# The first projection of a two-layer backbone, taken a quarter of the features at a time, and two pairs of modulation sums in one room

## The chip, the cores and the metric

The kernel runs on one core of one Trainium2 chip. The metric is device microseconds (us) of one execution. The kernel before took 1750.79 us, the median of three runs (1748.19 to 1751.60).

## What is computed

The reference is two layers of a diffusion backbone over 512 latent tokens `x` and 256 context tokens `ctx`, each of 1024 features in float32. The latents are modulated by a vector `c`, the context by another, `c_ctx`. Cut to the part that matters here:

```python
sc, scc = jax.nn.silu(c), jax.nn.silu(c_ctx)
m_lat = split(sc  @ mod_w[0] + mod_b[0], 6)      # six vectors of 1024: shift, scale, gate, twice
m_ctx = split(scc @ mod_w[0] + mod_b[0], 6)
h_ctx = rms(x_ctx) * norm_pre_mix * (1 + m_ctx[1]) + m_ctx[0]
h_lat = rms(x_lat) * norm_pre_mix * (1 + m_lat[1]) + m_lat[0]
h = concat([h_ctx, h_lat])                        # 768 tokens
gq, gk, gv, gog, gz, aq, ak, av = split(h @ w_in, (256, 256, 512, 512, 32, 512, 128, 128))
logit = gz[d] @ gla_w_gate[d] + gla_b_gate[d]     # d: forward, backward
g = log_sigmoid(logit) / 16                       # forget gates
# chunkwise gated linear recurrence in both directions over gq, gk, gv, g;
# softmax attention over aq, ak, av; both side by side through w_out
x_lat = x_lat + m_lat[2] * rms(o_lat @ w_out)
h_lat = rms(x_lat) * norm_pre_ffn * (1 + m_lat[4]) + m_lat[3]
# ... a gated FFN, and a second layer of another kind
```

## The kernel before

**Engines and tiles.** TensorE (PE) does the products and the transposes; VectorE (DVE) and ScalarE (ACT) move its results out of PSUM and do the element work; SyncE (SP) issues most loads. The dense products are float32 made of three products each: an operand X is split into a high part H (a cast, on ACT) and a low part L = X - H (a subtraction, on DVE), and `mm3` (above `gemm_T`) adds up H·H, H·L and L·H. A weight comes in 0.52 MB units: `unit` takes a `raw` tile (three of them), loads it on SP, casts it to `wH` (line 699, ACT) and makes `wL` (line 700, DVE); there are four `wH` and four `wL` for the whole program. PSUM has tiles by tag: two `mm` of 1024 columns, `sc0` and `sc1`, and two `tr` of 512.

**What sets the order.** Each engine takes its instructions in one list. A scheduler orders what isn't pinned; while `self.pinned` is set, what goes through `pin` (matmuls, transposes and what else is wrapped) keeps program order. Behind the head of the program that order is written by hand: each stage is a generator, and `run` steps them as a string of names says, one step for each name (`"Q Q e m"`). Buffers, PSUM tiles included, make the rest: who takes a tile waits until its last user is done.

**The head** (`run`, lines 1655 to 1706). `constants` loads the small vectors and turns them into columns `col` with one PE transpose, then makes `scT`, the two modulation vectors through silu. Six token tiles `xt` of 128 x 1024 are loaded, normed (sum of squares on ACT, scaling on DVE, line 1659) and transposed by PE into `xT` (eight blocks of 128 features by 768 tokens, copies at line 1666). Then two halves of the features follow: eight loads of `mod_w` (`mraw`, 128 x 1024, nine buffers), 32 narrow products into `mod_acc00`, four column groups side by side; `mod_cols` copies the rows out (line 485) and transposes them, and adds the bias (line 497); line 1694 makes the scale `aff01`; lines 1703 and 1705 apply shift and scale to that half of `xT`; `put` splits it into the high and low parts `x0`, `x1` of `h` (lines 665 and 666). Between the halves the units for the first product, 288 columns wide, are taken.

**The first layer's mixer** (`even_mixer`). Its first product `nat` computes the gate rank z (32 columns) and half of the queries for three pairs of token tiles, context first. `decays` transposes z and calls `gla_gates` (`logit`, then lines 1228 on). `mod_vec` computes the two next pairs of modulation vectors not on PE but on DVE: for each of eight 128-row slices of a weight, `macc = macc + mraw * scT` at line 554 (line 552 for the first slice), 128 x 1024, once for the latents and once for the context; then PE adds the 128 rows up with a column of ones (`mod_acc`), and `mod_cols` turns them into columns. The first pair, `macc020` and `macc021`, is the gate of the mixer; `gate_rows` makes its products with `norm_post_mix` and turns them into rows (`gc02` on line 600, `gt02` on line 606). The second pair, `macc030` and `macc031`, is the FFN's shift. Both pairs have accumulators of their own (`sums=4`), and the weight slices four buffers.

The string before the scan steps the q and k columns of the first two heads (`qk0`, evacuated as `gqk0`, `gqk2`), their values (`v0`, into `gvo`), the gates (`e`), modulation (`m`), the other queries (`q`) and keys with values (`kv`). The next string begins with the scan (`c0`, `l0`), whose first operands `arrg` are made on DVE (line 1248) and whose first product on PE is named `pcg`; between its steps stand the rest of `kv`, `qk1` and `v1`.

Of the kernel before, what the change touches and what calls it, by code (L numbers as in the profile page):

```python
# [17 lines left out]
P = 128  # L18
D = 1024
# [320 lines left out]
class Net:  # L340
# [3 lines left out]
    def __init__(self, ctx, tc, I, out):  # L344
        self.tc, self.nc, self.I, self.out = tc, tc.nc, I, out
        tc.nc.scalar.preload_act_table_set("silu_and_others")
# [41 lines left out]
    def constants(self):  # L388
# [11 lines left out]
        self.col_rows(  # L400
            "rows", 0, P, (
# [6 lines left out]

        nc.gpsimd.memset(self.scT, 0.0)
        nc.scalar.activation(  # L410
            self.scT[:, :, 0:2].rearrange("p k r -> p r k"),
            self.col[:, R_C : R_C + 16].rearrange("p (r k) -> p r k", r=2),
            AF.Silu,
        )
        self.modcol, self.gates = {}, {}

    def col_rows(self, nm, r0, r1, parts):

        rows = self.wp.tile([P, WU], F32, tag="mraw", bufs=2, name=nm)[: r1 - r0, :P]
        for at, src, n in parts:  # L420
            self.nc.scalar.dma_start(out=rows[at - r0 : at - r0 + n, :], in_=src)
        pt = self.tr_tile(f"pt_{nm}")
        self.tr(pt[:, 0 : r1 - r0], rows, self.ident[0 : r1 - r0, 0 : r1 - r0])
        self.nc.vector.tensor_copy(self.col[:, r0:r1], pt[:, 0 : r1 - r0])

    def late_constants(self):
        nc, I, cst = self.nc, self.I, self.cst
        self.col_rows(
            "rows2", R_NQM, R_END, (
# [10 lines left out]
        mf = self.wp.tile([P, WU], F32, tag="mraw", bufs=2, name="masks_f")[:, :160].rearrange("p (m i) -> p m i", m=5)  # L440
        nc.scalar.dma_start(out=mf, in_=I["const_masks"])
        nc.vector.tensor_copy(self.masks, mf)
# [30 lines left out]
    def mod_loads(self, l, ms, k, pool, bufs):  # L473
        us = []
        for m in ms:
            u = (pool or self.wp).tile([P, WU], F32, tag="mraw", bufs=bufs, name=f"mraw{l}{m}{k}")
# [54 lines left out]
    def mod_vec(self, pool, jobs, own=None, bufs=2, sums=2, single=False):  # L531
# [4 lines left out]
        load = lambda l, k, m: self.mod_loads(l, (m,), k, own, bufs)[0]  # L536
        u = load(*steps[0])
        i = 0
        for l, ms, then in jobs:
            self.mod_tiles(l, [m for m, r in ms if r == 0])  # L540
            accs = [pool.tile([P, D], F32, tag="macc", bufs=sums, name=f"macc{l}{m}{r}") for m, r in ms]
            while i < len(steps) and steps[i][0] == l and steps[i][2] in [m for m, _ in ms]:
                k, m = steps[i][1:]
                i += 1
                ahead = load(*steps[i]) if i < len(steps) else None
                here = [(a, r) for a, (mm, r) in zip(accs, ms) if mm == m]
                for x, (a, r) in enumerate(here):
# [3 lines left out]
                    if k == 0:  # L551
                        nc.vector.tensor_scalar(a, u, w, None, op0=ALU.mult)
# [505 lines left out]
    def even_mixer(self, h, mix, zu, last):  # L1058
# [24 lines left out]
        with self.tc.issue_after(last):  # L1083
            self.gemm_nat(w, 1536, 288, h, tiles, ev_z, us=zu)
# [779 lines left out]
```

## Time and profile before

| | before |
|---|---|
| median of three runs | 1750.79 us (1748.19 to 1751.60) |
| the profiled execution | 1749.34 us, of which its span is 1747.5 |
| mean granted TensorE clock | 0.993 of full speed |
| HBM read, written | 175.66 MB, 9.46 MB |
| first product of the mixer, first score of the scan | at 37.63 us and 133.98 us of the span |

All times inside the program are of the profiled execution and count from the start of its span. A row of the table by windows gives a stretch, its length, the busy time of PE, of its weight loads (PEld), DVE, ACT and POOL with the instruction counts in brackets, then the mean granted clock, the share of the time in which the 16 DMA engines were busy (a mean) and GB/s. A timeline row gives start, duration, engine, line, operation and tiles, and in square brackets the idle time just before it with what ended it. A row of the groups gives the count, the busy time in all, the mean in ns, and the idle time before. Line 371 is the helper through which every matmul and transpose passes, so PE's groups are told apart by their tiles. In "1328.47:1331.68 3.21, 0.01 (x1)" PE did 0.01 us of work in a stretch of 3.21 us.

### The profile page before, as it was taken

The numbers are of one execution on the slowest core, as the hardware profiler recorded it, in microseconds if no ns is written. First come the engines' busy times: TensorE is split into PE (matmuls) and PEld (weight loads), VectorE is DVE, ScalarE is ACT, GpSimd is POOL, SyncE is SP. The second block draws the span as 40 slices with busy tenths as digits, with TensorE's granted clock in tenths as the row PEclk, the third lists the DMA queues.
The fourth block names the chain that finished last, engine by engine and source line by source line (L and its number), as shares of the span: only waits on it lengthen the run. The fifth ranks groups of instructions, "written<-read, shape, count | busy, mean of one in ns | idle before, by whom it ended". The sixth has DMA issues, their size and how long they took to land. (4 is left out here: it accounts for less than half of the span.)

```text
span 1747.5 us, 32790 instructions
## 1 busy us (share of the span) xinstructions
PE 1700.9 (97%) x13732; PEld 1526.0 (87%) x13732; DVE 1280.9 (73%) x2036; ACT 857.8 (49%) x1473; POOL 74.2 (4%) x93
## 2 busy tenths in 40 slices
PE   6999999999999999999999999999999999999998
PEld 4889986788999989989998988889898899989997
DVE  5879658735966979787668658787764678878785
ACT  5545557746543333333347336666644664344342
POOL 1004100001000000000001000000000100000000
PEclk8999999999999999999999999999999999999999
DMA  8731013154322424332234752121114333233333
GB/s 318 222 112 39 3 39 107 36 156 139 113 90 73 153 77 156 109 110 61 73 123 143 262 160 63 48 62 50 50 62 133 121 98 108 86 102 106 99 106 120
DMA packets 169647, 187.23 MB, mean 107 GB/s; under 512 B 6262, under 2 KB 140956, under 8 KB 169500
## 3 DMA queue, kind: packets, MB, share of 16 engines
q1 hardware_dynamic: 167568, 181.56, 32.8%
q10 hardware_dynamic: 1932, 3.59, 0.7%
q8 instruction: 107, 1.75, 0.4%
q14 instruction: 40, 0.33, 0.1%
HBM read 175.66 MB, written 9.46 MB: 106 GB/s over the span
## 5 line engine op out<-in xcount | busy, mean ns | idle before, releaser
L371 PE MATMUL nat<-wH,x 128*128 128x256 f32 (+1 forms) x1216 | 229.0, 287 | 0.4 <-issue 0.4
L754 ACT CAST wH<-raw 128x1024 fp32r<-128x1024 f32 x120 | 124.5, 1051 | 197.2 <-PE acc L371 86.2
L700 DVE TENSOR_TENSOR wL<-raw,wH 128x1024 fp32r<-128x1024 f32 (+1 forms) x126 | 151.3, 1206 | 84.3 <-ACT wH L699 83.9
L371 PEld LDWEIGHTS nat<-wH,x 128*128 128x128 f32 x1216 | 193.3, 193 | 3.8 <-ACT y L1329 0.8
L755 DVE TENSOR_TENSOR wL<-raw,wH 128x1024 fp32r<-128x1024 f32 x120 | 145.2, 1221 | 64.9 <-ACT wH L754 64.8
L699 ACT CAST wH<-raw 128x1024 fp32r<-128x1024 f32 (+1 forms) x126 | 128.9, 1038 | 127.8 <-PE nat L371 34.4
L371 PE MATMUL nat<-wL,x 128*128 128x256 f32 (+1 forms) x608 | 173.4, 285 | 0.0
L371 PE MATMUL acc<-wH,gH 128*128 128x512 f32 x440 | 171.8, 390 | 0.0
L371 PE MATMUL acc<-wH,gL 128*128 128x512 f32 x440 | 171.5, 390 | 0.0
L371 PE MATMUL acc<-wL,gH 128*128 128x512 f32 x440 | 171.5, 390 | 0.0
L847 DVE TENSOR_TENSOR y<-y,acc 128x1024 f32<-128x1024 f32 x135 | 115.2, 863 | 37.0 <-PE acc L371 32.8
L554 DVE SCALAR_TENSOR_TENSOR macc<-mraw,scT,macc 128x1024 f32<-128x1024 f32 x98 | 122.6, 1277 | 10.7 <-DMA mraw<-in_mod_w_dram 10.4
L371 PE MATMUL ff<-x,wH 128*128 128x512 f32 (+1 forms) x512 | 127.6, 340 | 0.0
L624 POOL TENSOR_TENSOR rs<-ms,neghalf 128x1 f32<-128x1 f32 (+2 forms) x62 | 58.0, 937 | 1543.2 <-DVE ms L622 1543.1
L371 PEld LDWEIGHTS nat<-wL,x 128*128 128x128 f32 x608 | 117.3, 193 | 0.0
L371 PE MATMUL oproj<-wH,x 128*128 128x512 f32 x320 | 102.5, 397 | 3.2 <-ACT x L1270 3.2
L371 PEld LDWEIGHTS acc<-wH,gL 128*128 128x128 f32 x440 | 82.6, 188 | 17.3
L371 PEld LDWEIGHTS acc<-wH,gH 128*128 128x128 f32 x440 | 82.7, 188 | 16.6
L371 PEld LDWEIGHTS acc<-wL,gH 128*128 128x128 f32 x440 | 82.7, 188 | 16.5
L371 PEld LDWEIGHTS ff<-x,wH 128*128 128x128 f32 x512 | 87.3, 190 | 10.1
L955 ACT COPY qkh<-arr 128x512 f32<-128x512 f32 x112 | 70.1, 642 | 36.3 <-DVE arr L960 32.1
L371 PE MATMUL ff<-x,wL 128*128 128x256 f32 (+1 forms) x256 | 86.2, 337 | 0.0
(344 smaller groups left out, 4047.2 us busy)
## 6 DMA issues: line engine op xcount, KB each, us to landing
mraw<-in_mod_w_dram SPq DMA_DIRECT2D x96, 512.0 KB, 4.8
raw<-in_ffn_w_gate_dram SPq DMA_DIRECT2D x44, 512.0 KB, 3.7
raw<-in_ffn_w_up_dram SPq DMA_DIRECT2D x44, 512.0 KB, 3.8
raw<-in_ffn_w_down_dram SPq DMA_DIRECT2D x44, 512.0 KB, 3.6
raw<-in_odd_w_in_dram SPq DMA_DIRECT2D x40, 512.0 KB, 3.7
raw<-in_even_w_in_dram SPq DMA_DIRECT2D x16, 512.0 KB, 4.6
x<-xr SPq DMA_DIRECT2D x14, 512.0 KB, 2.6
xr<-x SPq DMA_DIRECT2D x14, 512.0 KB, 8.1
```

The costliest lines, as they stand in the source:

```text
L371: return self.pin(self.nc.tensor.matmul(*a, **k))
L554: nc.vector.scalar_tensor_tensor(a, u, w, a, op0=ALU.mult, op1=ALU.add)
L624: nc.gpsimd.tensor_tensor(rs, ms, self.neghalf.to_broadcast([P, w]), op=ALU.pow)
L699: nc.scalar.copy(H[:, :m], raw[:, :m])
L700: nc.vector.tensor_tensor(L[:, :m], raw[:, :m], H[:, :m].bitcast(F32), op=ALU.subtract)
L754: self.nc.scalar.copy(H, f)
L755: self.nc.vector.tensor_tensor(L, f, H.bitcast(F32), op=ALU.subtract)
L847: nc.vector.tensor_tensor(y, y, pt, op=ALU.add)
L955: nc.scalar.copy(qkv[:, :, :, half, :], dst)
```

## The change

**The head by quarters.** The six token tiles move from the pool of the head into a pool of their own, `xr`: four rooms of tag `x0` for the latents, two of tag `x1` for the context. Their norms run two tiles ahead of their transposes; the transposes of the constants (`finish`, `late`) and the load of the silu table come later than before. Matmuls, transposes and the casts marked with `pin` keep program order from here on. `begin_loads` takes a quarter of the modulation weights (256 features of shift and of scale, in two tiles of 128 x 2048, rows of 1 KB), `begin_weights` a quarter of the rows of the projection's columns for `gqk0`, `gqk2` and `v0` as one unit of 128 x 1024. `begin` then goes through the quarters: `sums` is the 32 narrow products, now 128 wide, `columns` the transpose, bias, `aff01`, shift, scale and split of that quarter's two feature blocks, `across` the products for `gqk0` and `gqk2`, `values` those for `v0`, and `gates` the gate rank z as 64 narrow products, 32 rows by 192 columns, into free columns of `gqk0`'s PSUM tile. All five PSUM tiles (two `mm`, `sc0`, `sc1`, one `tr`) hold their sums through the four quarters; `md`, for the modulation, is `sc0` ahead of quarter one and the other `tr` after that. When the quarters are done, `even_mixer` copies them out, and the queries that stood first (`Q`) come next, with the weights `wq` taken in quarter four.

**The second pair of sums.** `mod_vec` now starts inside the quarters, with three loads ahead (`deep=3`), its weight slices in the rooms of tag `x0`, and its two accumulators in those of tag `x1` (`sums=2`): the second pair takes the room of the first. Its additions are pinned. The string before the scan is rewritten, `mods` is run to its end before the scan begins, and one `m` behind the first `l0` is replaced by `qk1`.

```diff
-    def even_mixer(self, h, mix, zu, last):
+    def begin_loads(self, pp, q):
+        us = []
+        for i in range(2):
+            u = pp.tile([P, 4, 2, 256], F32, tag="mraw", bufs=5, name=f"mraw0{q}{i}")
+            src = self.I["mod_w"][0, 512 * i : 512 * i + 512, 0:2048].rearrange("(k p) (m f) -> p k m f", p=P, m=2)
+            for m in (1, 0):
+                self.nc.sync.dma_start(out=u[:, :, m], in_=src[:, :, m, 256 * q : 256 * q + 256])
+            us.append(u)
+        return us
+
+    def begin_weights(self, q):
+
+        nc = self.nc
+        w = self.I["even_w_in"][0][256 * q : 256 * q + 256, :].rearrange("(k p) m -> p k m", p=P)
+        raw = self.wp.tile([P, WU], F32, tag="raw", bufs=3, name="raw")
+        H, L = (self.wp.tile([P, WU], F32R, tag=f"w{x}", bufs=4, name=f"w{x}") for x in "HL")
+        rv = raw.rearrange("p (k n) -> p k n", k=2)
+        for at, c0, n in ((0, 0, 128), (128, 256, 128), (256, 512, 256)):
+            nc.sync.dma_start(out=rv[:, :, at : at + n], in_=w[:, :, c0 : c0 + n])
+        nc.scalar.copy(H, raw)
+        nc.vector.tensor_tensor(L, raw, H.bitcast(F32), op=ALU.subtract)
+        return [x.rearrange("p (k n) -> p k n", k=2) for x in (H, L)]
...
+        ws[1] = self.begin_weights(1)
+        z = pp.tile([P, KD, 32], F32, name="zw")
+        nc.sync.dma_start(out=z, in_=I["even_w_in"][0][:, 1536:1568].rearrange("(k p) m -> p k m", p=P))
+        late = self.late_constants(pp)
+        md = self.sc_tile("md", 0)
+        rows = sums(0, us[0], md)
+        columns(0, rows, md)
+        md = self.tr_tile("md")
+        v = [self.sc_tile("v0", 0), self.sc_tile("v0", 1), self.tr_tile("v0")]
+        v = {t0: x.rearrange("p (a n) -> p a n", a=2) for t0, x in zip((4, 0, 2), v)}
+        qk = [self.mm_tile(f"gqk{x}") for x in (0, 2)]
+
+        def across(q, x, tok):
+            for k in range(2):
+                W = [y[:, k, 128 * x : 128 * x + 128] for y in ws[q]]
+                three(qk[x][:, tok], W, h.hl(2 * q + k, tok), 2 * q + k)
+
+        def values(q, t0):
+            for a in range(2):
+                tok = slice((t0 + a) * P, (t0 + a + 1) * P)
+                for k in range(2):
+                    three(v[t0][:, a, :], h.hl(2 * q + k, tok), [y[:, k, 256:512] for y in ws[q]], 2 * q + k, a == 0)
+
+        def gates(ks):
...
+        lat, ctx = slice(0, 512), slice(512, 768)
+        for q in range(4):
+            if q < 2:
+                us[q + 2] = self.begin_loads(pp, q + 2)
+                ws[q + 2] = self.begin_weights(q + 2)
+            if q == 2:
+                mods = self.mod_vec(
+                    xr, ((0, ((2, 0), (2, 1)), (2, R_NQM)), (0, ((3, 0), (3, 1)), None)), xr, 4, 2, tags=("x1", "x0"), deep=3
+                )
+            if q == 3:
+                wq = [self.nat_units(I["even_w_in"][0], 1568, 256, half)[0] for half in range(2)]
+            across(q, 0, ctx)
+            across(q, 1, ctx)
+            values(q, 4)
+            if q in (1, 2):
+                rows = sums(q + 1, us[q + 1], md)
+            if q == 3:
+                gates(range(4, 8))
+                for _ in range(2):
+                    next(mods)
+            across(q, 0, lat)
+            if q in (1, 2):
+                columns(q + 1, rows, md)
+            across(q, 1, lat)
+            if q == 0:
+                rows = sums(1, us[1], md)
+            values(q, 0)
+            if q == 0:
+                columns(1, rows, md)
+            values(q, 2)
+            if q == 1:
+                gates(range(4))
+            if q == 2:
+                for _ in range(2):
+                    next(mods)
+        return qk, v, wq, mods, late
```

`sums`, `columns` and `gates` are not shown; in `columns` the two splits and the affine of a quarter are pinned, first for the context and then for the latents. The rest of the change, in `even_mixer`, `mod_vec` and `run`:

```diff
-    def mod_vec(self, pool, jobs, own=None, bufs=2, sums=2, single=False):
...
-        load = lambda l, k, m: self.mod_loads(l, (m,), k, own, bufs)[0]
-        u = load(*steps[0])
+        load = lambda l, k, m: self.mod_loads(l, (m,), k, own, bufs, tags[1])[0]
+        us = [load(*x) for x in steps[:deep]]
...
-            accs = [pool.tile([P, D], F32, tag="macc", bufs=sums, name=f"macc{l}{m}{r}") for m, r in ms]
+            accs = [pool.tile([P, D], F32, tag=tags[0], bufs=sums, name=f"macc{l}{m}{r}") for m, r in ms]
+                if i + deep < len(steps):
+                    us.append(load(*steps[i + deep]))
                 i += 1
-                ahead = load(*steps[i]) if i < len(steps) else None
+                u = us.pop(0)
...
+        for g in range(4):
+            self.pin(nc.vector.tensor_copy(zT[:, 192 * g : 192 * g + 192], pq[32 * g : 32 * g + 32, 768:960]))
+        nc.scalar.mul(gqk[0], pq[:, :NT], 0.125)
+        nc.scalar.copy(gqk[1], pk[:, :NT])
+        for t0 in tiles:
+            nc.scalar.copy(gv[:, t0 : t0 + 2, 0:256], pv[t0])
+        late()
...
-        run("qk0 qk0 e m qk0 e e v0 qk0 e e m qk0 e e m v0 e e m m q v0 m m v0 m m kv q m m q m q m m m m m m m m m qk1 kv m")
+        run("Q Q e e m Q e e m Q q e e m q e e m m q m m q kv m m kv m m")
+        for _ in mods:
+            pass
         tp.release()
+        xr.release()
         gp = self.open_pool("gla")
-        run("c0 l0 kv m c0 kv c0 v1 qk1 c0 p p qk1 c0 l0 p qk1 l0 c0 g0 qk1 l0 p c1 p v1 l0 p v1 l0 c1 p v1 l0 c1 l1 g1 g0 c1 g0 r0 c1 l1 r0 g0 l1")
+        run("c0 l0 qk1 kv c0 kv c0 v1 qk1 c0 p p qk1 c0 l0 p qk1 l0 c0 g0 qk1 l0 p c1 p v1 l0 p v1 l0 c1 p v1 l0 c1 l1 g1 g0 c1 g0 r0 c1 l1 r0 g0 l1")
...
+        xr = self.open_pool("xr", "right")
         with self.pool("pre0") as pp:
             xT = pp.tile([P, KD, NT], F32, name="xT")
+            self.pinned = True
+            xs = {t: xr.tile([P, D], F32, tag=f"x{int(t >= LT)}", bufs=2 if t >= LT else 4, name=f"xt{t}") for t in order}
             for t in order:
-                xt = pp.tile([P, D], F32, tag="xt", bufs=6, name=f"xt{t}")
-                nc.sync.dma_start(out=xt, in_=xin(t))
-                rs = self.rstd(self.sumsq(xt), D)
-                nc.vector.tensor_scalar(xt, xt, rs, None, op0=ALU.mult)
+                nc.sync.dma_start(out=xs[t], in_=xin(t))
+            us, ws = {0: self.begin_loads(pp, 0)}, {}
...
+            norm(order[0])
+            norm(order[1])
+            for i, t in enumerate(order):
+                if i + 2 < len(order):
+                    norm(order[i + 2])
+                turn(t)
+                if i == 1:
+                    finish()
+                if i == 3:
+                    ws[0] = self.begin_weights(0)
+            begun = self.begin(pp, xr, h, xT, us, ws)
```

**What moves.** The first place is DVE behind the last token transposes. `xT` are those copies, `wL` a weight's low part, `modrows` the sums on their way to the transpose, `modcol00` shift and `modcol01` scale. Before:

```order
L1666 COPY xT_103<-xT21_208 128x4x128
L1666 COPY xT_103<-xT31_230 128x4x128
L485 COPY modrows_288<-mod_acc000_239 128x256
L497 TENSOR_TENSOR modcol00_236<-modT_290,col_84 128x4 x2
L497 TENSOR_TENSOR modcol01_237<-modT_290,col_84 128x4 x2
L700 TENSOR_TENSOR wL_300<-raw_298,wH_299 128x576
L1694 SCALAR_TENSOR_TENSOR aff01_238<-modcol01_237,col_84 128x2x4
L700 TENSOR_TENSOR wL_306<-raw_304,wH_305 128x576
L1705 TENSOR_SCALAR xT_103<-xT_103,aff01_238,modcol00_236 128x256 x4
```

After; `raw_221` is the projection's unit for quarter one, `raw_262` that for quarter two, whose loads are issued behind both quarters' modulation weights:

```order
L1838 COPY xT_102<-xT21_235 128x4x128
L1838 COPY xT_102<-xT31_247 128x4x128
L1093 TENSOR_TENSOR wL_223<-raw_221,wH_222 128x1024
L1093 TENSOR_TENSOR wL_264<-raw_262,wH_263 128x1024
L1118 COPY modrows_316<-md_283 128x128
L1128 TENSOR_TENSOR modcol01_254<-md_283,col_83 128x2x2
L1128 TENSOR_TENSOR modcol00_253<-md_283,col_83 128x2x2
L1133 SCALAR_TENSOR_TENSOR aff01_255<-modcol01_254,col_83 128x2x2
L1142 TENSOR_SCALAR xT_102<-xT_102,aff01_255,modcol00_253 128x256
L1145 TENSOR_TENSOR x1_325<-xT_102,x0_324 128x2x256
```

The low parts of both units stand ahead of the first quarter's `modrows`; before, the two low parts stood behind it. On ACT the casts `wH_222` and `wH_263` stand ahead of the first affine; the two casts of before stood there too.

The second place is ACT around the query weights and the copies of the first products. Before; `nat_569` is a tile of the first product, `wH_748` and `wH_927` are casts of later weights:

```order
L1080 COPY zn_465<-nat_569 128x64
L1081 COPY natq_452<-nat_569 128x8x64
L699 CAST wH_748<-raw_747 128x1024
L699 CAST wH_927<-raw_926 128x1024
L1133 ACTIVATE gqk0_458<-gqk0_653 128x768
L1228 ACTIVATE am_725<-logit00_723,col_84 128x256
L1228 ACTIVATE am_734<-logit01_732,col_84 128x256
```

After, behind the last split of quarter four (`x2`); `wH_1064` and `wH_1070` are the casts of the query weights `wq`:

```order
L1144 CAST x2_326<-xT_102 128x2x512
L714 CAST wH_1064<-raw_1063 128x1024
L714 CAST wH_1070<-raw_1069 128x1024
L1249 COPY gqk2_826<-gqk2_339 128x768
L1251 COPY gvo_821<-v0_335 128x2x256
L1248 ACTIVATE gqk0_825<-gqk0_338 128x768
L1251 COPY gvo_821<-v0_336 128x2x256
```

Two casts of loads now stand ahead of the copies that free the PSUM tiles of the quarters; before, `gqk0` had its copy between other work, after the first query tile was out.

The third place is DVE ahead of the scan's first operand `arrg`. Before, the last of the second pair's sums (`macc030`, `macc031`) and what follows:

```order
L700 TENSOR_TENSOR wL_1052<-raw_1050,wH_1051 128x1024
L700 TENSOR_TENSOR wL_1058<-raw_1056,wH_1057 128x1024
L554 SCALAR_TENSOR_TENSOR macc030_1185<-mraw036_1257,scT_79,macc030_1185 128x1024
L554 SCALAR_TENSOR_TENSOR macc031_1186<-mraw036_1257,scT_79,macc031_1186 128x1024
L554 SCALAR_TENSOR_TENSOR macc030_1185<-mraw037_1261,scT_79,macc030_1185 128x1024
L554 SCALAR_TENSOR_TENSOR macc031_1186<-mraw037_1261,scT_79,macc031_1186 128x1024
L485 COPY modrows_1117<-mod_acc_1112 128x512
L497 TENSOR_TENSOR modcol02_690<-modT_1119,col_84 128x8 x2
L600 TENSOR_TENSOR gc02_1126<-modcol02_690,col_84 128x16
L606 COPY gt02_1180<-gcT02_1178 16x128
L700 TENSOR_TENSOR wL_1276<-raw_1274,wH_1275 128x1024
L485 COPY modrows_1272<-mod_acc_1267 128x512
```

After, from the first pair's end on:

```order
L499 COPY modrows_1226<-mod_acc_1221 128x512
L511 TENSOR_TENSOR modcol02_708<-modT_1228,col_83 128x8 x2
L615 TENSOR_TENSOR gc02_1235<-modcol02_708,col_83 128x16
L715 TENSOR_TENSOR wL_1453<-raw_1451,wH_1452 128x1024
L621 COPY gt02_1301<-gcT02_1299 16x128
L568 TENSOR_SCALAR macc030_1306<-mraw030_1009,scT_78 128x1024
L568 TENSOR_SCALAR macc031_1307<-mraw030_1009,scT_78 128x1024
L570 SCALAR_TENSOR_TENSOR macc030_1306<-mraw031_1094,scT_78,macc030_1306 128x1024
L570 SCALAR_TENSOR_TENSOR macc031_1307<-mraw031_1094,scT_78,macc031_1307 128x1024
L570 SCALAR_TENSOR_TENSOR macc030_1306<-mraw032_1167,scT_78,macc030_1306 128x1024
L570 SCALAR_TENSOR_TENSOR macc031_1307<-mraw032_1167,scT_78,macc031_1307 128x1024
L570 SCALAR_TENSOR_TENSOR macc030_1306<-mraw033_1308,scT_78,macc030_1306 128x1024
```

The second pair's sums, slices 0 to 7 and 16 instructions in all, begin behind `gt02` now (nine more follow these rows, up to `mraw037`); before, all 16 were ahead of the first pair's `modrows`. On PE, `gt02`'s transpose `gcT02` stands between two products of the keys with 48 matmuls each, and the second pair's `mod_acc` behind the second of these.

More of the change, by code (lines that the diff above doesn't have):

```diff
@@ L399, in constants @@
         self.modb = self.col[:, R_MB : R_MB + 96]
-        self.col_rows(
-            "rows", 0, P, (
+        turned = self.col_rows(
+            self.wp.tile([P, WU], F32, tag="mraw", bufs=2, name="rows")[:, :P], "rows", 0, P, (
                 (R_C, I["c"].rearrange("o (k p) -> (o k) p", p=P), 8),
@@ L529, in mod_group, with mod_vec @@
         turned()
-    def mod_vec(self, pool, jobs, own=None, bufs=2, sums=2, single=False):
+    def mod_vec(self, pool, jobs, own=None, bufs=2, sums=2, single=False, tags=("macc", "mraw"), deep=1):
         nc = self.nc
         steps = [(l, k, m) for l, ms, _ in jobs for k in range(KD) for m in sorted({m for m, _ in ms})]
-        load = lambda l, k, m: self.mod_loads(l, (m,), k, own, bufs)[0]
-        u = load(*steps[0])
+        load = lambda l, k, m: self.mod_loads(l, (m,), k, own, bufs, tags[1])[0]
+        us = [load(*x) for x in steps[:deep]]
         i = 0
@@ L1059, in even_mixer @@
+    def even_mixer(self, h, mix, begun, xr):
         nc, I = self.nc, self.I
@@ L1073, in even_mixer @@
         gqk = [mixg.tile([P, NT], F32, tag=f"gqk{x}", bufs=1, name=f"gqk{2 * x}") for x in range(2)]
+        (pq, pk), pv, wq, mods, late = begun
         og = [p.tile([P, NTT, 256], F32, name=f"og{c}") for c, p in enumerate((mixg, mix))]
         tp = self.open_pool("gate")
-        zn = tp.tile([P, NTT, 32], F32, name="zn")
         zT = tp.tile([32, NT], F32, name="zT")
-        def ev_z(t0, pt):
-            nc.scalar.copy(zn[:, t0 : t0 + 2, :], pt[:, :, 0:32])
-            nc.scalar.copy(q_part(0)[:, t0 : t0 + 2], pt[:, :, 32:288].rearrange("p t (m e) -> p t m e", m=4))
-        with self.tc.issue_after(last):
-            self.gemm_nat(w, 1536, 288, h, tiles, ev_z, us=zu)
+        for g in range(4):
+            self.pin(nc.vector.tensor_copy(zT[:, 192 * g : 192 * g + 192], pq[32 * g : 32 * g + 32, 768:960]))
[4 more added lines that the diff above has]
+        late()
         wg = tp.tile([32, 2, 256], F32, name="wg")
@@ L1114, in nat, with queries, ev_q @@
                 yield
-        def ev_q(t0, pt):
-            nc.scalar.copy(q_part(1)[:, t0 : t0 + 2], pt[:, :, :256].rearrange("p t (m e) -> p t m e", m=4))
+        def queries(n, us=None):
+            def ev_q(t0, pt):
+                nc.scalar.copy(q_part(n)[:, t0 : t0 + 2], pt[:, :, :256].rearrange("p t (m e) -> p t m e", m=4))
+            return nat(1536 + 32 + 256 * n, ev_q, us)
         def ev_kv(t0, pt):
             nc.scalar.copy(natk[:, t0 : t0 + 2, :], pt[:, :, :256])
-        gq, gk, ends = {}, {}, {}
+        gq, gk, ends = {0: gqk[0]}, {0: gqk[1]}, {}
         def qk(c):
@@ L1130, in qk @@
                     if g is groups[-1]:
-                        t = gqk[x // 2] if c == 0 else mixg.tile([P, NT], F32, tag=f"gqk{x // 2}", bufs=1, name=f"gqk{x}")
+                        t = mixg.tile([P, NT], F32, tag=f"gqk{x // 2}", bufs=1, name=f"gqk{x}")
                         if x < 2:
```

176 lines of the change are left out of this document (99 added, 77 removed).

## The prediction

> **What bounds the kernel now.** I read the page first: the span, and which engine fills it.
>
> ```profile
> span 1747.5 us, 32790 instructions
> PE 1700.9 (97%) x13732; PEld 1526.0 (87%) x13732; DVE 1280.9 (73%) x2036; ACT 857.8 (49%) x1473; POOL 74.2 (4%) x93
> ```
>
> TensorE is busy 97% of the time, so the change can win where PE idles or runs at half clock, and lose where it makes PE wait. Next the table by windows (length, busy time and instructions of PE, PEld, DVE, ACT, POOL, then clock, DMA share, GB/s), which shows the head of the program and some stretches used below:
>
> ```profile
> 0.00:20.00 20.00, 10.70 (x57) 7.21 (x58) 7.88 (x17) 10.90 (x19) 5.07 (x15) 1.00 0.94 349
> 20.00:40.00 20.00, 15.17 (x136) 6.87 (x136) 11.54 (x33) 9.29 (x18) 0.52 (x1) 0.71 0.90 319
> 24.00:34.00 10.00, 6.25 (x56) 1.32 (x50) 7.79 (x21) 5.91 (x12) 0.52 (x1) 0.71 1.05 387
> 37.63:42.16 4.53, 4.53 (x22) 4.53 (x20) 4.10 (x15) 2.84 (x7) 0.00 (x0) 0.53 0.45 121
> 62.00:66.00 4.00, 4.00 (x27) 3.42 (x26) 3.43 (x4) 1.05 (x1) 0.00 (x0) 1.00 1.00 315
> 120.00:140.00 20.00, 20.00 (x283) 18.86 (x282) 19.25 (x48) 16.92 (x40) 6.96 (x4) 1.00 0.22 64
> 1328.47:1331.68 3.21, 0.01 (x1) 0.01 (x1) 1.13 (x2) 2.18 (x4) 0.00 (x0) 1.00 0.57 203
> 1332.16:1335.57 3.41, 3.41 (x14) 2.52 (x13) 3.27 (x5) 2.27 (x4) 0.00 (x0) 0.50 0.53 154
> ```
>
> For 38 us the DMA engines are full and PE only transposes tokens and adds up modulation. The PE timeline shows where the dense work begins:
>
> ```profile
> 35.67 1.08 PE L371 MATMUL mod_acc<-mraw,scT 128*32 128x256 f32 x8 [0.26 <-DMA mraw<-in_mod_w_dram]
> 37.30 0.69 PE L374 MATMUL modT<-ident,modrows 128*128 128x128 f32 x2 [0.55 <-DVE modrows L485]
> 37.63 0.59 PE L371 MATMUL nat<-wH,x 128*128 128x288 f32 x1
> ```
>
> The last sum waits for its load, and 37.63 is the first product of the projection. The other end of the changed stretch is the first score of the scan (`pcg`); behind it the order on PE is the old one, so I compare the time of `pcg`. PE timeline:
>
> ```profile
> 106.08 1.06 PE L371 MATMUL mod_acc<-macc,one 128*32 128x512 f32 x8
> ...
> 108.66 0.66 PE L374 MATMUL modT<-ident,modrows 128*128 128x128 f32 x4 [1.52 <-DVE modrows L485]
> ...
> 133.98 0.33 PE L371 MATMUL pcg<-gqk,gqk 64*32 64x32 f32 x16
> ```
>
> From 37.63 to 133.98 are 96.35 us with 1.52 us of idle time.
>
> **The head.** Six tokens of 0.52 MB make 3.15 MB. The first 20 us moved 20 x 349 = 6.98 MB; what followed the tokens came at 387, so they were through at 20 - 3.83/0.387 = 10.1. Now a quarter of the modulation weights (2.10 MB) and of the projection's (0.52 MB) follows, twice, before the second `raw` is there: 5.24 MB, in pieces of 1 KB and less. The nearest row for such pieces is 62 to 66 us, full share at 315 GB/s: 17.0 us with the small constants; the other bound is 387, 13.9. From last piece to use I add 2.2: the last sum of before had 12.13 MB ahead of it, which ends at 33.3 by the same rates, and ran at 35.67. So this `raw` lands at 29.3 (26.2 at best).
>
> That matters because of the first order excerpt: casting the **second** quarter's weights stands on ACT and DVE ahead of the **first** quarter's columns. Both engines wait there, with everything behind them, until 29.3. Then come the cast, the low part, and the chain of columns, by these DVE rows and the groups of DVE and ACT (busy, mean ns, idle):
>
> ```profile
> 24.41 0.42 DVE L485 COPY modrows<-mod_acc 128x256 f32<-128x256 f32 x1 [1.62 <-DMA mraw<-in_mod_w_dram]
> 25.43 0.37 DVE L497 TENSOR_TENSOR modcol<-modT,col 128x4 f32<-128x4 f32 x4 [0.59 <-PE modT L374]
> ...
> 26.38 0.16 DVE L1694 SCALAR_TENSOR_TENSOR aff<-modcol,col 128x8 f32<-128x8 f32 x1
> ```
>
> ```profile
> L554 DVE SCALAR_TENSOR_TENSOR macc<-mraw,scT,macc 128x1024 f32<-128x1024 f32 x28 | 34.4, 1273 | 0.0
> L700 DVE TENSOR_TENSOR wL<-raw,wH 128x1024 fp32r<-128x1024 f32 x10 | 12.2, 1220 | 5.8 <-ACT wH L699 5.7
> ...
> L552 DVE TENSOR_SCALAR macc<-mraw,scT 128x1024 f32<-128x1024 f32 x4 | 2.9, 747 | 0.0
> L485 DVE COPY modrows<-mod_acc 128x512 f32<-128x512 f32 x2 | 1.4, 688 | 0.2 <-PE mod_acc L371 0.2
> ...
> L606 DVE COPY gt<-gcT 16x128 f32<-16x128 f32 x1 | 0.3, 278 | 5.4 <-PE gcT L374 5.4
> ```
>
> ```profile
> L699 ACT CAST wH<-raw 128x1024 fp32r<-128x1024 f32 x1 | 1.0, 1045 | 0.0
> ...
> L1136 ACT COPY gqk<-gqk 128x768 f32<-128x768 f32 x1 | 0.8, 777 | 0.0
> L1142 ACT COPY gvo<-nat 128x512 f32<-128x512 f32 x1 | 0.6, 587 | 1.3 <-PE nat L371 1.3
> ```
>
> 1.05 + 1.22 + 0.42 + 0.4 (transpose) + 0.37 + 0.16 + 0.5 (scale) + 0.6 (cast, as `gvo`) = 4.7: first product at **34.0** (31 to 35), 3.6 earlier than now. The norms two tiles ahead and the later table load end long before and are costed at nothing: the load of the second `raw` covers them; without it the first `raw`, at 20.6, would still be later than the tokens.
>
> **The quarters.** Products by their windows (PE alone; the last two rows are the sums of four `gqk` and four `logit` stretches):
>
> ```profile
> 37.63:58.89 21.26, 21.26 (x144) 0.90 0.58 184
> 88.61:106.10 17.49, 17.49 (x144) 1.00 0.56 174
> ```
>
> ```profile
> sum 17.28, PE 17.27; mean PE 4.32
> ```
>
> ```profile
> sum 5.93, PE 5.92; mean PE 1.48
> ```
>
> The same `qk0` and `v0` cost 17.3 + 17.5 = 34.8. The cold start stays: 22 products in 4.53 us at clock 0.53 instead of some 2.9, 1.7 lost. Modulation of quarters two to four now stands between products: 64 records each, half as wide as the 102 records that took 10.1 us with waits, at about 62 ns when not waiting; by width 2.0 a quarter, and 4.0 if width didn't count. I take 2.3, so 6.9, and 0.6 for transposes. The gate rank z as 64 narrow records: 3.0 in all. Ahead of quarter two, `wL` of quarter four stands on DVE between affine and scale: columns, `wL`, scale, cast, low part make 3.5, of which 12 products (1.5) hide part: 2.0. Sum 49.0; the quarters end at 83.0.
>
> **The hold at their end.** The query product needs the PSUM of `gqk0`. On ACT the cast of a weight whose buffer PE frees only with the last product of quarter four stands ahead of the copies (second excerpt): 1.05 + 0.78 + 0.59 + 0.78 = 3.2 of waiting. A wait of 3.21 at 1328.47 was followed by 3.4 us at clock 0.50, 1.7 lost; I take half of that here, 0.85. Products resume, in effect, at 87.0.
>
> [...]
>
> **The second pair of sums.** Seven products of 48 (5.83 each, 40.8), the logits 5.9, the first pair's `mod_acc` to next product 3.0 as now, 0.5 of small waits: the product of `kv`'s first tile ends at 137.2. Before, the second pair had accumulators of its own and DVE ran it from 82.7, between other work. Now it uses the first pair's room, and all 16 additions stand behind the copy `gt` (third excerpt), which waits for PE's `gcT` after the product before: DVE is free at 137.2 - 5.8 + 0.6 = 132.0. They take 14 x 1.23 + 2 x 0.73 = 18.7, to 150.7. PE stands at `mod_acc` from 137.2: **13.5 us** idle, and the later key product, the scan and all else queue behind it on PE and DVE. Then `wL` 1.22, `modrows` 0.69, transposes 0.5, the last product 5.83, and a cold spell of 1.7: `pcg` at **160.6**, 26.6 later than 133.98.
>
> The scan's first operand is made here:
>
> ```profile
> 123.72 0.42 DVE L1248 TENSOR_TENSOR arrg<-gqk,glaf 128x256 f32<-128x256 f32 x1
> ```
>
> Now it is 10.3 us ahead of `pcg`, then about 8, in a stretch where DVE is busy 19.25 of 20. I take 0.5 for that, bounded by 0 and 5.
>
> Sum: 26.6 + 0.5 = 27.1. The profiled run took 1749.34 (span 1747.5), so 1776.4; the runs' median, 1750.79, lies 1.45 above the profiled run, hence **1777**.
>
> **Rivals.**
>
> *No early hold* (0.10). If the second `raw` were there in time, the first would decide: 20.6 + 4.7 = 25.3, 8.7 earlier, 1768. For it: the DMA share of 0.94 leaves some room. Against: it asks 2.6 MB to arrive in no time.
>
> *DVE stays behind in the scan* (0.09). All 2.3 us of lost lead, and more where PE waits for DVE, with the narrow sums at 4.0: 5.1 + 5, about 1787. For it: 19.25 of 20. Against: DVE idles 5.4 at `gt` and 5.7 at `wL` before.
>
> *The head isn't shortened* (0.04). Were the loads so slow that products begin at 37.63 as now, 3.6 more: 1780.
>
> *Ready work passes waiting work* (0.05, the faster side). If on DVE and ACT an instruction with its operands there could pass one that waits, the early hold (8.7), `wL` of quarter four (1.2), the hold at the quarters' end (3.2 + 0.85) and PE's wait for sums with its cold spell (13.5 + 1.7) would go: 29.2 less, 1748. It decides as soon as the 16 additions start 13.5 us before `gt`. Against it: the DVE groups' instructions ran before in the order in which the program lists them, `gt` with 5.4 us of idle time ahead of it included. [...]
>
> **How the numbers follow.** The forecast has 0.72. Its bounds: head -3/+1, sums -1/+5, hold -4/+1, cold spells -2.5/0, lag -0.5/+4.5, seldom all at once: 1767 to 1786. The range takes in the rival at 1768 and reaches to 1764 and 1787. What a measurement can tell here is about 0.2%, 3.5 us. All cases but one lie far above that: slower 0.93; of the last rival's 0.05 and the unforeseen, faster 0.05, same 0.02.
>
> **What would show it.** In the profile after: first `gqk` product near 34, with DVE and ACT idle for DMA `raw` before it; a PE wait of about 3 us for ACT `gqk0` near 83; PE idle 12 to 15 us at `mod_acc` for DVE `macc`, and a half-clock slice behind it; `pcg` near 160. If PE waits less than 5 us at that `mod_acc`, or the products start before 28, I'm wrong.

## The result, and the profile after

The changed kernel takes 1774.63 us (median of four runs, 1773.87 to 1775.82) against 1750.30 (1748.19 to 1751.60): a ratio of 1.0141, with an interval of 1.0123 to 1.0158. It is slower, by 1.4%. The profiled execution took 1773.87 us. Its page begins:

```profile
span 1772.1 us, 33157 instructions
PE 1702.5 (96%) x13918; PEld 1532.0 (86%) x13918; DVE 1283.1 (72%) x2030; ACT 856.9 (48%) x1462; POOL 73.4 (4%) x93
```

PE has 1.6 us more work in a span that is 24.6 longer: what was added is waiting. The PE timeline gives the ends of the changed stretch and its longest waits, and the window behind them the rest of the scores:

```profile
32.96 0.47 PE L373 MATMUL md<-ident,modrows 128*128 128x128 f32 x1 [8.71 <-DVE modrows L1118]
35.23 1.30 PE L370 MATMUL gqk<-x,wH 128*128 128x256 f32 x2 [1.79 <-ACT x L1144]
...
85.49 0.39 PE L370 MATMUL nat<-wH,x 128*128 128x256 f32 x1 [1.76 <-ACT gqk L1249]
...
121.14 1.40 PE L370 MATMUL mod_acc<-macc,one 128*32 128x512 f32 x8
...
147.85 2.17 PE L370 MATMUL mod_acc<-macc,one 128*32 128x512 f32 x6 [12.26 <-DVE macc L570]
...
159.69 0.25 PE L370 MATMUL pcg<-gqk,gqk 64*32 64x32 f32 x6
```

```profile
135.59:147.85 12.26, 0.00 (x0) 0.03 (x1) 12.26 (x12) 1.19 (x3) 0.00 (x0) 0.61 0.41 131
147.85:153.00 5.15, 4.35 (x14) 1.70 (x15) 4.26 (x9) 1.58 (x4) 0.00 (x0) 0.50 0.34 104
159.69:253.20 93.51, 92.89 (x1917) 87.25 (x1916) 76.85 (x202) 54.40 (x119) 28.11 (x22) 1.00 0.06 19
```

In the first window PE does nothing and DVE is busy all the time; in the second PE is back, at half clock. The first dense product starts 2.40 us earlier than before (35.23 against 37.63), the first score 25.71 later (159.69 against 133.98), so the stretch between grew by 28.1. The scan's scores, from the first to the last, took 93.12 before:

```profile
133.98:227.10 93.12, 92.95 (x1917) 87.31 (x1916) 74.04 (x197) 52.00 (x112) 27.14 (x22) 1.00 0.07 20
```

That is 0.4 more now. Some 1.5 us came back behind it, where the order on PE is the old one; no run tells why, and the changed kernel's own runs differ by 2 us.

The groups of PE from 35 to 84 us say what the quarters hold beside the products (count, busy time, mean in ns, idle time before):

```profile
L370 PE MATMUL md<-mraw,scT 128*32 128x128 f32 x192 | 5.9, 274 | 0.0
L370 PE MATMUL gqk<-xT,zw 128*32 128x192 f32 x64 | 3.0, 329 | 0.0
L373 PE MATMUL md<-ident,modrows 128*128 128x128 f32 x3 | 0.8, 272 | 0.0
```

Of the 28.1 us, 12.3 are the wait at `mod_acc` and some 3.4 the half clock behind it (from `mod_acc` to the end of the next product 11.8 us, 147.85 to 159.69; for the first pair 8.4, 121.14 to 129.58), 5.9 and 0.8 the sums and transposes of quarters two to four, which before ran while PE had to wait for loads anyway (3.7 us in seven waits for `mraw`), and 3.4 the waits ahead of quarter two (1.29 and 0.34) and at the quarters' end (1.76). That makes 25.8. The 2.3 us that are left are not split further; the z products (3.0) are in them, against the 32 columns less of the first query product.

### The profile page after: what moved, and what is told of

It is laid out like the page before. It is cut to its first block, busy times and chain, and to the rows that moved or that the text cites. A ratio compares the mean times of both kernels' runs of the same rounds, so it can differ in the third digit from the quotient of the medians.

```text
span 1772.1 us, 33157 instructions
## 1 busy us (share of the span) xinstructions
PE 1702.5 (96%) x13918; PEld 1532.0 (86%) x13918; DVE 1283.1 (72%) x2030; ACT 856.9 (48%) x1462; POOL 73.4 (4%) x93
## 5 line engine op out<-in xcount | busy, mean ns | idle before, releaser
L769 ACT CAST wH<-raw 128x1024 fp32r<-128x1024 f32 x120 | 124.5, 1051 | 195.6 <-DVE y L862 70.7
L370 PE MATMUL nat<-wH,x 128*128 128x256 f32 x1120 | 209.4, 286 | 1.8 <-ACT gqk L1249 1.8
L715 DVE TENSOR_TENSOR wL<-raw,wH 128x1024 fp32r<-128x1024 f32 x120 | 146.8, 1229 | 85.6 <-ACT wH L714 85.2
L770 DVE TENSOR_TENSOR wL<-raw,wH 128x1024 fp32r<-128x1024 f32 x120 | 145.1, 1220 | 64.5 <-ACT wH L769 64.3
L714 ACT CAST wH<-raw 128x1024 fp32r<-128x1024 f32 x120 | 124.3, 1051 | 123.0 <-PE nat L370 29.6
L370 PEld LDWEIGHTS nat<-wH,x 128*128 128x128 f32 x1120 | 177.4, 193 | 5.4 <-ACT gqk L1249 2.0
L370 PE MATMUL nat<-wL,x 128*128 128x256 f32 x560 | 159.0, 284 | 0.0
L570 DVE SCALAR_TENSOR_TENSOR macc<-mraw,scT,macc 128x1024 f32<-128x1024 f32 x98 | 122.2, 1277 | 8.3 <-DMA mraw<-in_mod_w_dram 7.9
L370 PEld LDWEIGHTS nat<-wL,x 128*128 128x128 f32 x560 | 108.0, 193 | 0.0
```

Source lines behind the costliest of these rows:

```text
L370: return self.pin(self.nc.tensor.matmul(*a, **k))
L570: self.pin(nc.vector.scalar_tensor_tensor(a, u, w, a, op0=ALU.mult, op1=ALU.add))
L714: nc.scalar.copy(H[:, :m], raw[:, :m])
L715: nc.vector.tensor_tensor(L[:, :m], raw[:, :m], H[:, :m].bitcast(F32), op=ALU.subtract)
L769: self.nc.scalar.copy(H, f)
L770: self.nc.vector.tensor_tensor(L, f, H.bitcast(F32), op=ALU.subtract)
```

## The experiments

Each run stands beside runs of the kernel before on the same chip; "first score" is the first `pcg` of its profile (159.69 in the changed kernel). The head ends at different times from one profile to the next: with the head as changed, the first dense product started between 32.9 and 35.2 us in six profiles of such kernels, so first scores alone tell differences of some 2 us at best. The kernel before took 1750.0 to 1752.8 us beside these runs (medians), so a difference between the times of two runs is uncertain by some 2 us as well, and the ratios say more.

**The room or the list?** The prediction said that the additions stand late because they use the first pair's room. Two edits separate the two: room of its own, and no pin.

```diff
+            if self.room and then is None:
+                accs = [x.rearrange("p t n -> p (t n)")[:, :D] for x in self.room]
...
+        self.room = og
```

> The changed kernel, but the second pair of modulation sums gets room of its own (the two gate tiles og0 and og1, which nothing uses until later), and nothing else is edited. Theory 1, as in the prediction, that the shared room keeps the additions back: they start as early as their loads allow, TensorE's wait of 12.3 us at the second mod_acc and its half-clock spell of about 3.4 go, 1759 us. Theory 2, that the pinned order in VectorE's list keeps them back: the list is the same as without the edit (the 16 additions behind the copy gt02), so the wait is still 12 us and the time 1774 within 3.

Measured: 1775.52 us (1771.95 to 1780.36), ratio to before 1.0138 (1.0115 to 1.0162). On DVE and PE:

```profile
133.33 0.27 DVE L625 COPY gt<-gcT 16x128 f32<-16x128 f32 x1
133.53 1.39 DVE L572 TENSOR_SCALAR og<-mraw,scT 128x1024 f32<-128x1024 f32 x2
134.85 16.81 DVE L574 SCALAR_TENSOR_TENSOR og<-mraw,scT,og 128x1024 f32<-128x1024 f32 x14
```

```profile
150.61 1.07 PE L371 MATMUL mod_acc<-og,one 128*32 128x512 f32 x2 [12.26 <-DVE og L574]
```

The additions had room of their own and still began behind `gt`, and the wait is the same 12.26 us. Theory 1 falls: it is the place in the list.

```diff
+                free = self.pin if then else (lambda x: x)
...
-                        self.pin(nc.vector.scalar_tensor_tensor(a, u, w, a, op0=ALU.mult, op1=ALU.add))
+                        free(nc.vector.scalar_tensor_tensor(a, u, w, a, op0=ALU.mult, op1=ALU.add))
```

> The changed kernel with the room still shared, but the second pair's additions no longer pinned, so the scheduler puts them from just ahead of modrows of the first pair on, at about 123 us instead of 130.8. Theory 1 (the room): they can't start before the first mod_acc has read the room, at 122.5; 18.7 us of additions plus 3 of other work end near 144.5, wait 8 us instead of 12.3, 1769 us. Theory 2 (the pin alone): the wait would go nearly whole, 1760.

Measured: 1765.12 us (1764.58 to 1765.56), ratio 1.0077 (1.0062 to 1.0092).

```profile
139.50 1.07 PE L370 MATMUL mod_acc<-macc,one 128*32 128x512 f32 x2 [4.45 <-DVE macc L571]
```

4.45 us of wait are left, 9.5 us of time are won (24.3 us above the kernel before beside it in the changed kernel, 13.2 here: 11.1 by that). Without the pin the room does hold the additions back, until the first `mod_acc` has read it: DVE stands idle for 0.81 us for it, and the first addition runs at 121.39. The result lies about halfway between the two theories, 8 us of wait and 1769, or next to none and 1760.

> The changed kernel with both: room of its own for the second pair, and its additions not pinned. The scheduler then puts 6 of the 16 additions ahead of the first pair's modrows and the rest between what follows. If room and pin together hold the additions back: the last ten take 12.3 us from 123 on, plus 2.5 of other work, to 138, the wait is 2 to 3 us, the time 1762 (1759 to 1766). If VectorE has no time for them earlier anyway (it is busy 72 per cent of the span): the wait stays above 8, 1770.

Both edits: 1766.20 us (1761.87 to 1769.68), ratio 1.0083 (1.0058 to 1.0108). PE no longer waits at the second `mod_acc`, and the first score comes at 146.5, but the scores then take 96.1 us instead of 93.5:

```profile
146.50:242.60 96.10, 94.41 (x1917) 88.78 (x1916) 79.61 (x206) 54.24 (x117) 28.75 (x23) 0.98 0.09 24
```

Part of what the wait gave up is paid in the scan; the time is no better than without room of its own.

**Room and pin kept, the list changed.** The first pair's sums start one quarter earlier; nothing else.

```diff
-            if q == 2:
+            if q == 1:
                 mods = self.mod_vec(
...
-            if q == 2:
-                for _ in range(2):
+            if q in (1, 2):
+                for _ in range(5 - q):
                     next(mods)
```

> The changed kernel with its shared room and its pinned additions, but the first pair's sums begin one quarter earlier: four of the eight slices behind quarter two's products, three behind quarter three's, one in quarter four, instead of two and two in the last two quarters. The strings of steps are the same, so the second pair's additions are listed between the query products, behind the first pair's end at about 105 us, and are over by 125, ahead of the second mod_acc at about 136. If the place in the list is what cost the time, room and pin may stay: the wait of 12.3 us and the half-clock spell of 3.4 behind it go, 1759 us (1757 to 1762). If a shared room costs time wherever it is used: above 1766.

Measured: 1765.10 us (1765.06 to 1766.41), ratio 1.0085 (1.0071 to 1.0099). The wait at the second `mod_acc` is 2.2 instead of 12.3 with room and pin as they were, so what the wait cost goes for the most part with both kept. The additions didn't begin near 105, as expected: they still stand behind `gt`, from 121.65 to 141.6. But `gt` now comes 16.8 us before PE gets to the second `mod_acc` (121.45 and 138.29), in the changed kernel 5.0 (130.56 and 135.59). The time is still 6 us above what was expected; beside the 2.2 us left, a new wait came on DVE and PE in quarter three:

```profile
65.54 7.26 DVE L570 SCALAR_TENSOR_TENSOR macc<-mraw,scT,macc 128x1024 f32<-128x1024 f32 x6
72.72 0.28 DVE L1118 COPY modrows<-md 128x128 f32<-128x128 f32 x1
```

```profile
73.06 0.33 PE L373 MATMUL md<-ident,modrows 128*128 128x128 f32 x1 [1.94 <-DVE modrows L1118]
```

Four slices are more than DVE can fit ahead of the next quarter's `modrows`.

**The same in the kernel before**, where nothing of it is pinned:

```diff
-(0, ((3, 0), (3, 1)), None)), tp, 3, 4)
+(0, ((3, 0), (3, 1)), None)), tp, 3, 2)
```

> The kernel before with one edit: the second pair shares the first pair's two accumulators. Nothing is pinned there. The scheduler then lists 16 additions from the first pair's modrows on. If the room alone costs time: they run from 107.2 to about 130 (18.7 plus 4 of other work), TensorE waits some 9 us at the second mod_acc at 120.9 and runs a half-clock spell, 1762 us (1758 to 1765). If the room costs nothing without the pin: 1751.

Measured: 1759.87 us (1758.19 to 1762.53), ratio 1.0053 (1.0039 to 1.0067). The wait at the second `mod_acc` was 4.46 us, half of what I expected, and the first score 6.7 later. A shared room alone costs some 9 us there: DVE stands idle for 3.96 us until the first `mod_acc` has read the room, and the additions run from 106.77 to 125.9, beyond 120.43, where PE gets to the second `mod_acc`.

**Is it PE's idle time that costs?** One product of the keys is moved ahead of the second `mod_acc`, into the wait.

```diff
-        run("Q Q e e m Q e e m Q q e e m q e e m m q m m q kv m m kv m m")
+        run("Q Q e e m Q e e m Q q e e m q e e m m q m m q kv m m kv m m kv")
...
-        run("c0 l0 qk1 kv c0 kv c0 v1 qk1 c0 p p qk1 c0 l0 p qk1 l0 c0 g0 qk1 l0 p c1 p v1 l0 p v1 l0 c1 p v1 l0 c1 l1 g1 g0 c1 g0 r0 c1 l1 r0 g0 l1")
+        run("c0 l0 qk1 c0 kv c0 v1 qk1 c0 p p qk1 c0 l0 p qk1 l0 c0 g0 qk1 l0 p c1 p v1 l0 p v1 l0 c1 p v1 l0 c1 l1 g1 g0 c1 g0 r0 c1 l1 r0 g0 l1")
```

> The changed kernel with one product of the keys, 48 matmuls that stood behind the second mod_acc, moved ahead of it. The additions end where they did, at 148.9. If TensorE's idle time is all that the wait costs: 6 of its 12.3 us are filled, 1769 us. If the scan's operands on VectorE, which also stand behind the additions (first one at 151.5, the rest over the next 6 us), then set its start: 1772 or more.

Measured: 1776.20 us (1772.04 to 1778.46), ratio 1.0132 (1.0117 to 1.0147), as without the edit. The wait is halved, and it came back between the scores:

```profile
149.83 1.07 PE L370 MATMUL mod_acc<-macc,one 128*32 128x512 f32 x2 [6.41 <-DVE macc L570]
...
154.78 0.44 PE L370 MATMUL pcg<-gqk,gqk 64*32 64x32 f32 x16
...
156.64 0.44 PE L370 MATMUL pcg<-qkg 64*32 64x32 f32 x16 [1.21 <-ACT qkg L970]
158.50 0.28 PE L370 MATMUL pcg<-qkg 64*32 64x32 f32 x4 [1.41 <-ACT qkg L970]
```

From `gt` on DVE to the last score passed 122.2 us here (132.63 to 254.84) and 122.6 in the changed kernel (130.56 to 253.18). PE stands at `pcg` for the copies `qkg` of ScalarE, and the first of these stands 1.65 us for `arrg` from DVE, which comes at 153.60, behind the additions, `wL` and `modrows`. So it is DVE's list that sets the scan's start, and PE's wait at `mod_acc` only shows it. (Another 2.0 us of wait in the scan are for `gvo` from ScalarE, 0.6 in the changed kernel.)

One more thing is held there: ScalarE's own operand copy `arrg` of 512 columns waits for the second `mod_acc`, 13.03 us in the changed kernel and 7.19 here. In `own_room` it doesn't wait (it runs at 139.49, ahead of the `mod_acc` at 150.61) and the time is the same, so this copy isn't what delays the scan in the changed kernel; and in `kv_ahead` it runs at 151.84, ahead of DVE's `arrg` at 153.60.

**The early hold.** Quarter two's unit is taken behind the first quarter's columns.

```diff
         us[1] = self.begin_loads(pp, 1)
-        ws[1] = self.begin_weights(1)
...
         columns(0, rows, md)
+        ws[1] = self.begin_weights(1)
```

> The changed kernel, but the projection's unit for quarter two is taken behind the first quarter's columns, so that neither ScalarE nor VectorE waits for its load ahead of them. If that early wait holds the first products: they start near 26.5 instead of 35.2, quarters two to four follow without new waits since their loads end by 44 us, and the time falls by 7.5 to 8.7, to 1766. If the loads set the pace of the quarters anyway, the start is earlier but the quarters end where they did, near 83.5, and the time is 1774 within 2.

Measured: 1769.23 us (1768.84 to 1773.74), ratio 1.0107 (1.0089 to 1.0124). The first product starts at 26.29, 8.9 earlier, but the same hold comes one quarter later, for quarter three's unit:

```profile
38.03 1.04 ACT L1092 CAST wH<-raw 128x1024 fp32r<-128x1024 f32 x1 [6.67 <-DMA raw<-in_even_w_in_dram]
```

```profile
40.59 0.47 PE L373 MATMUL md<-ident,modrows 128*128 128x128 f32 x1 [2.87 <-DVE modrows L1118]
```

The next run takes all units behind the columns, gives quarter one the order of the others, and copies the first products out ahead of the next casts (with an edge in the scheduler from each cast to the copy):

```diff
-                ws[q + 2] = self.begin_weights(q + 2)
...
-            if q in (1, 2):
+            if q < 3:
                 columns(q + 1, rows, md)
+            if q < 2:
+                ws[q + 2] = self.begin_weights(q + 2)
```

> The run late_unit carried on, with the sums of the second pair left as the change has them: each quarter's projection unit is taken behind the columns of the quarter ahead of it, quarter one's order is made that of the others, and ScalarE copies the first products out ahead of the next query casts. From the trace of late_unit (first score at 153.5): the wait of 2.9 for the unit of quarter three goes, the wait of 1.6 ahead of quarter two goes, and of the 1.8 at the quarters' end about 1 goes; first score near 148, 1764 us. If these waits only uncover loads that are late anyway: 1768.

Measured: 1761.41 us (1760.71 to 1762.96), ratio 1.0063 (1.0050 to 1.0075), 13.2 less than the changed kernel. Of the three waits in the expectation, that of 1.6 ahead of quarter two was gone in `late_unit` already; the other two are gone here (first score at 147.1 instead of 153.5). The second `mod_acc` waits 12.26 as before.

**Both together.** The edits of `early_sums` and `head_order` in one kernel:

> The edits of early_sums and head_order in one kernel. If they add up: 1774.6 - 15.7 - 10.9, 1748 us (1745 to 1752), the same as the kernel before within what can be told: the quarters give up with the 5.9 us of modulation sums between products most of what the earlier start gains. If VectorE, with all additions in the stretch ahead of the scan, falls behind in it: 1754 or more.

Measured: 1754.84 us (1749.92 to 1760.33), ratio 1.0026 (1.0015 to 1.0038): not the 1748 that was expected. The gains measured in the two runs, 9.5 and 13.2, would give 1751.9; the 3 us between that and 1754.84 are too few to say that the gains don't add up, since each ratio is known to some 0.15%. What was missing is in good part that `early_sums` had won 9.5 and not 15.7. DVE's four slices hold `modrows` here too (2.24 us of wait), and the second `mod_acc` waits 2.21. Then three, three and two slices in quarters two, three and four, and the second pair not pinned:

```diff
-                for _ in range(5 - q):
+                for _ in range(3):
...
+                free = self.pin if then else (lambda x: x)
```

> The run both_moves with its two remaining waits taken out: three slices of the first pair's sums in quarter two, three in quarter three and two in quarter four (before 4, 3, 1), so that VectorE reaches modrows of quarter four in time (2.2 us of wait and some 1.5 at half clock behind it), and the second pair's additions not pinned, so that they start ahead of the copy gt02 (2.2 us of wait at the second mod_acc). If the waits were the whole of what it lost: first score at 131 instead of 136.9, 1749 us. If VectorE's total work ahead of the scan is what counts: the waits shift into the scan, 1753 or more.

Measured: 1748.22 us (1746.90 to 1749.81) beside 1752.75 of the kernel before on this chip, ratio 0.9974 (0.9963 to 0.9984): the one version with all its work that beats both kernels, by a little more than a measurement can tell. Its profile doesn't show where: its first score, at 133.98, comes when it does before. It is the slowest of its eight runs, and the profile of before is below its median, so I leave that open. In it PE waits once more, by way of ScalarE for `zT`, which stands behind ten additions on DVE:

```profile
66.35 12.04 DVE L571 SCALAR_TENSOR_TENSOR macc<-mraw,scT,macc 128x1024 f32<-128x1024 f32 x10
78.31 1.44 DVE L1245 COPY zT<-gqk 32x192 f32<-32x192 f32 x4
```

```profile
79.78 0.81 ACT L1246 ACTIVATE gqk<-gqk 128x768 f32<-128x768 f32 x1 [6.86 <-DVE zT L1245]
```

```profile
81.66 0.67 PE L370 MATMUL logit<-zT,wg 32*128 32x256 f32 x2 [2.26 <-ACT gvo L1250]
```

What do the sums between products cost in it? They are cut to one eighth, so this kernel leaves out most of these sums:

```diff
+            first = KD - 1 if q else 0
-            for k in range(KD):
+            for k in range(first, KD):
```

> The run both_trim with 7 of 8 slices left out of the modulation sums of quarters two to four (so shift and scale of these features lack most of their sum); all loads stay. It measures what these sums cost between the products: 3 x 1.95 x 7/8, 5.1 us less than both_trim, if TensorE sets the pace there; nothing, if the loads or the columns' chain do.

Measured: 1746.95 us (1745.28 to 1751.26), ratio 0.9973 (0.9963 to 0.9984), not told apart from `both_trim`. The first score is 3.1 earlier (130.84), but `modrows` of quarter four and the first `logit` wait 2.07 and 2.48 for DVE. Its first-pair additions stand there.

Last, the two last slices behind `zT` and room of its own for the second pair:

```diff
                 gates(range(4, 8))
-                for _ in range(2):
-                    next(mods)
...
+            if self.room and then is None:
+                accs = [x.rearrange("p t n -> p (t n)")[:, :D] for x in self.room]
```

> The run both_trim with the second pair in room of its own (the two gate tiles) and the last two slices of the first pair's sums behind the copies zT, which both_trim had behind all of them: TensorE's logit waited 2.3 us for zT there, with some 1.5 us at half clock behind it. The scheduler now lists the second pair's additions between the logit steps from 75 us on. If that wait is what is left to win: first score 3.8 earlier, near 130, and 1744.5 us. If VectorE's total work ahead of the scan sets the scan's start: the score may be earlier, but the time stays at 1748.

Measured: 1750.46 us (1747.38 to 1753.92), ratio 0.9990 (0.9979 to 1.0001). The wait at `logit` is gone, and another stands 28 us later:

```profile
109.36 0.47 PE L374 MATMUL modT<-ident,modrows 128*128 128x128 f32 x1 [3.43 <-DVE modrows L500]
```

`modrows` came behind additions and gate work on DVE. The first score came at 137.99, 4.0 later than in `both_trim` and not 3.8 earlier; 2.9 of that is a later first product (29.04 against 26.12). The time isn't better than that of `both_trim`.

## Why the prediction was right, and where it was not

*Sign and size* were right: 1777 forecast, 1774.63 measured; for the profiled execution 1776.4 and 1773.87. (The sum as written, 1776.4 and 1.45, gives 1777.9 and not 1777.) That the first score came within 0.9 us is luck in part: the first product was 1.2 late and the half clock behind the sums 1.7 longer than I had it, the hold at the quarters' end 2.2 shorter and the wait for the sums 1.2 shorter.

*The head.* Right in mechanism: ACT and DVE stood idle for the second `raw` ahead of the first quarter's columns.

```profile
30.40 1.04 ACT L1092 CAST wH<-raw 128x1024 fp32r<-128x1024 f32 x1 [7.85 <-DMA raw<-in_even_w_in_dram]
```

It landed at 30.4 instead of 29.3, so the first product came at 35.23 instead of 34.0, outside my bounds of 31 to 35 by 0.2. `late_unit` shows the hold: without it the start is 8.9 earlier (I had 8.7).

*The quarters* ended at 83.65 (83.0). The sums took 5.9 for three quarters (6.9), z 3.0 (3.0), the waits at the start of quarter two, behind `wL` of quarter four, 1.6 (2.0).

*The hold at their end* was over-sized: 1.76 instead of 3.2 + 0.85. Only the second of the two casts was late, and the query product took the PSUM tile of `gqk2`, whose copy stands right behind it; I had added three copies. ACT:

```profile
83.70 1.04 ACT L714 CAST wH<-raw 128x1024 fp32r<-128x1024 f32 x1 [9.08 <-PE v L370]
84.65 0.79 ACT L1249 COPY gqk<-gqk 128x768 f32<-128x768 f32 x1
```

The words ahead of the second order excerpt are also wrong in one point: the two casts are not those of `wq` but of the next query weights (`q`).

*The second pair of sums.* PE stood at `mod_acc` from 135.6 (137.2) to 147.9 (150.7), 12.3 us (13.5). The first score came at 159.69 (160.6). The half clock behind the wait cost some 3.4 where I had 1.7.

*Two steps of the reasoning failed*, though their numbers came out. The prediction put it: "Now it uses the first pair's room, and all 16 additions stand behind the copy `gt`." `own_room` shows that the room was not what put them there: with room of their own they stand in the same place, and `early_sums` takes 10 us of the wait away with room and pin kept. The cause is where the steps list them; the pin keeps the scheduler from moving them up, and when it may (`free_order`), the room is the next limit. And I priced the wait along PE's chain, as idle time of PE with a spell behind it, though I had named DVE's queue beside PE's. `kv_ahead` shows that filling half of the wait wins nothing, because the scan's operands stand behind the additions on DVE too. The forecast held all the same, because its number came from the listed place and not from the room, and because PE's idle time and DVE's lateness are the same 12 us here.

*The lag in the scan* was 0.4 (0.5). *The rivals:* the early hold did occur; products began before 37.63; DVE did not fall further behind in the scan in the changed kernel, but did in `own_free` (2.6 us). Ready work did not pass waiting work: DVE stood idle for 4.94 us behind the waiting `wL`, up to 129.42. The additions, listed behind `gt`, had their room free by then (the first `mod_acc` ended at 122.54), and in `free_order`, where they are listed earlier, they run from 121.39 on.

```profile
129.42 1.23 DVE L715 TENSOR_TENSOR wL<-raw,wH 128x1024 fp32r<-128x1024 f32 x1 [4.94 <-ACT wH L714]
130.56 0.27 DVE L621 COPY gt<-gcT 16x128 f32<-16x128 f32 x1
130.76 1.39 DVE L568 TENSOR_SCALAR macc<-mraw,scT 128x1024 f32<-128x1024 f32 x2
```

The norms two tiles ahead were not tried by themselves.

## What to carry to other kernels

Where an engine takes its work in order, as DVE did here (4.94 us idle behind a waiting `wL`), look at what stands ahead of the first instruction that others wait for: here a cast for the next quarter, and 16 additions behind a small copy, cost more (8.9 us of a later start by `late_unit`, a wait of 12.26) than the earlier start won (2.40). Before giving a wait to a shared buffer, give the work a buffer of its own and see whether its place in the list moves. And before filling an engine's idle time, see whether what comes behind the wait stands on the same late engine: it did in `kv_ahead`, where the wait fell from 12.26 to 6.41 us, and the time was 1776.20 beside 1774.63.

## What the runs showed of the hardware

The half clock came with a shorter wait than the 3.21 us of the kernel before: in `both_trim` PE's only idle time from 75 to 90 us was the 2.26 ahead of `logit`, and the clock in that stretch was 0.89, with 1.00 in the 15 us on either side. The wait at the quarters' end, 1.76 us in the changed kernel, was followed by full clock in the changed kernel and in `late_unit` (1.00 in the 6.00 and 5.90 us of the 48 products behind it), and by 1.5 us more for the same 48 products in `own_room`, `free_order` and `own_free` (0.77 in 7.50 us); the windows of the changed kernel and of `free_order` over these products:

```profile
85.40:91.40 6.00, 5.91 (x48) 5.81 (x48) 3.23 (x14) 3.71 (x7) 0.00 (x0) 1.00 0.73 217
```

```profile
83.10:90.60 7.50, 7.44 (x49) 7.30 (x49) 3.21 (x14) 3.69 (x7) 0.00 (x0) 0.77 0.57 177
```

If the rest ran at full clock, a mean of 0.77 over 7.50 us is some 3.45 us at half clock, an estimate (7.50 x 0.23 / 0.5). What decides between the two outcomes is not shown. These are different kernels, each profiled once: that one kernel's own runs differ by this 1.5 us is not shown either.
